# A router kernel fed by one stream of loads: spare products before four rows, an earlier table load, and a regrouped end of the stream

## The chip, the cores and the metric

The kernel runs on one core of a Trainium2 chip. The metric is the device time of one execution in microseconds (us); lower is better. A core has several engines that run side by side: TensorE (PE) multiplies matrices, with its weight loads shown apart as PEld; VectorE (DVE) and ScalarE (ACT) do elementwise work; GpSimd (POOL) here issues nearly all loads; SyncE (SP) here waits for loads and issues the stores. They are tied together by semaphores.

## The reference

```python
batch, seq, dim = 16, 512, 1024
num_loras = 8
# x: (16, 512, 1024) fp32, router_weights: (1024, 8) fp32

def reference(x, router_weights):
    logits = np.matmul(x, router_weights)
    exp_logits = np.exp(logits - np.max(logits, axis=-1, keepdims=True))
    return (exp_logits / np.sum(exp_logits, axis=-1, keepdims=True)).astype(np.float32)
```

x has 8192 rows of 1024 numbers, 33.5 MB in fp32. Each row is multiplied with an 8-column matrix and a softmax is taken over the 8 results. There is little arithmetic for each byte that is read.

## The kernel before

The 8192 rows are spread over 128 partitions, 64 to each. What the kernel and this text call "row j" is the j-th of these on every partition: a block of 128 rows of x. Row blocks 0 to 3 come in one fp32 load on the SyncE queue and are cast by ScalarE; blocks 4 to 62 come on the GpSimd queue in loads of several blocks, cast to bf16 by the DMA on the way; block 63 comes in three pieces of columns.

```python
    LOADS = [4] + [8] * 4 + [4] * 4 + [2, 2, 2] + [1] * 5     # blocks per load
    PIECES = [4, 2, 2]                                        # of block 63, in units of 128 columns
    G, SKIP = 8, 4
    TRIPS = 31
    ...
    place = [16640]                                           # next free address in SBUF
    ...
    X_AT = place[0]
    xa = sb("x_all", [P, J, D], bf16)
    x_f32 = sb("x_f32", [P, LOADS[0], D], fp32)
```

SyncE passes the landing of each load on, as a count of blocks that PE may take (semaphore s_in). GpSimd issues the loads one after the other, and they queue up:

```python
    for i, r in enumerate(LOADS):
        if i:
            sp.wait_ge(s_ld[i], 16)
            sp.sem_inc(s_in, r)
    ...
    for i, r in enumerate(LOADS):
        if i:
            nc.gpsimd.dma_start(
                out=xa[:, first[i]:first[i] + r, :], in_=x_rows[:, first[i]:first[i] + r, :]
            ).then_inc(s_ld[i], 16)
```

PE turns each block with eight transposes (through the identity) into PSUM. DVE copies five of the eight turned pieces to SBUF, ACT copies three, and PE multiplies them with the weights. PE runs this as a loop over two blocks. It turns the next block before it multiplies the present one, takes its instructions in order, and computes two "filler" products of 128x512 per trip whose result nobody reads:

```python
    def loop_turn(b):
        pe.wait_ge(s_in, 1).then_inc(s_in, -1)    # has the block landed?
        for c in range(KO):
            t = again(turn_like, ...)              # transpose at the address in register r_x[c]
            ...
        for c in range(KO):
            ...
            pe.reg_add(r_x[c], r_x[c], D * 2)      # on to the next block

    def fill():
        return pe.matmul(spare, lhsT=filler[:, 0:P], rhs=filler, start=True, stop=True)
    ...
    with nc.body("rows_multiply", valid_engines=only_pe):
        fill()
        fill()
        multiply(1, None)
        pe.br("rows_turn")
    with nc.body("rows_turn", valid_engines=only_pe):
        loop_turn(1)
        multiply(0, None)
        loop_turn(0)
        pe.br_lt(r_x[0], left_of(TRIPS - 1), on_true="rows_multiply", on_false="rows_done")
```

ScalarE waits for the first load before anything else. The load of its function table isn't written out here; it comes with the first cast and so stands behind that wait:

```python
    act.wait_ge(s_f, 16).then_inc(s_f, -16)
    for i in range(2):
        cast(i)
        for j in (2 * i, 2 * i + 1):
            act_copy(j, j)
```

After the loop, blocks 60 to 63 are finished alone: two multiplies, the three pieces of block 63, four small softmaxes, one last store.

Of the kernel before, what the change touches and what calls it, by code (L numbers as in the profile page):

```python
# [11 lines left out]
def kernel(  # L12
# [6 lines left out]
    nc = tc.nc  # L19
    P = 128  # L20
    B, S, D = x.shape
# [10 lines left out]
    fp32 = mybir.dt.float32  # L32
    bf16 = mybir.dt.bfloat16
    Exp = mybir.ActivationFunctionType.Exp
    X = mybir.AxisListType.X
    ALU = mybir.AluOpType

    LOADS = [4] + [8] * 4 + [4] * 4 + [2, 2, 2] + [1] * 5  # L40
    PIECES = [4, 2, 2]
    G, SKIP = 8, 4
    TRIPS = 31
# [5 lines left out]
    DONE = ends[-1]  # L49
    assert sum(LOADS) == J - 1 and sum(PIECES) == KO and ends[-1] == J - ALONE  # L50
    VN, SN = 5, 3

    place = [16640]

    def sb(name, shape, dtype):
        size = mybir.dt.size(dtype)
        for n in shape[1:]:
            size *= n
        at = place[0]
        place[0] = -(-(at + size) // 64) * 64  # L60
        return nc.alloc_sbuf_tensor_at(name, shape, dtype, offset=at).ap()
# [1 line left out]
    def ps(name, shape, dtype):  # L63
        return nc.alloc_psum_tensor(name, shape, dtype).ap()

    X_AT = place[0]
    xa = sb("x_all", [P, J, D], bf16)
    x_f32 = sb("x_f32", [P, LOADS[0], D], fp32)
    identity = sb("identity", [P, P], bf16)
    ident = sb("ident", [P, P], fp32)  # L70
    w8 = sb("w8", [KO, P, N], fp32)
# [31 lines left out]
    s_w = nc.alloc_semaphore("s_w")  # L103
    s_ld = [sem(f"s_ld{i}") for i in range(len(LOADS))]
    s_z = [sem(f"s_z{i}") for i in range(len(PIECES))]
# [21 lines left out]

    first = [sum(LOADS[:i]) for i in range(len(LOADS))]
    cols = [sum(PIECES[:i]) for i in range(len(PIECES))]


    with tc.manual_schedule():
        early = [
            nc.sync.dma_start(out=x_f32, in_=x_rows[:, 0:LOADS[0], :]).then_inc(s_f, 16),
            nc.scalar.dma_start(
# [25 lines left out]

    for j in range(LOADS[0]):
        sp.wait_ge(s_cast, j + 1)
# [34 lines left out]
    pe = nc.tensor  # L198
    r_x = [pe.alloc_register(f"rx{c}") for c in range(KO)]
    r_l = pe.alloc_register("rl")  # L200
    for c, r in enumerate(r_x):

        pe.reg_mov(r, X_AT + D * 2 + c * P * 2 + (P - 1) * 2)
    pe.reg_mov(r_l, LG_AT + 256 * (SKIP - 1))

    def at(ap, like, r):
        return mybir.RegisterAccessPattern(
            ap=ap, dtype=like.dtype, memsetref=like.tensor.name + "_set",
            regref=r.name, is_regloc_offset=False, reg_ap_offset=r.name,
            const_ap_offset=0, const_sub_tensor_id=0,  # L210
        )

    def again(like, **k):
        return pe.add_instruction(copy.replace(like, name=f"I-{nc.next_id()}", **k))

    def turn_ap(b, c):
        return (ptv if c < VN else pts)[b][:, c if c < VN else c - VN, :]

    def chunk(b, c):
        return xTv[b][:, c, :] if c < VN else xTs[b][:, c - VN, :]  # L220

    def loop_turn(b):

        pe.wait_ge(s_in, 1).then_inc(s_in, -1)  # L224
        for c in range(KO):
            t = again(
                turn_like,
                ins=(turn_like.ins[0], at([[J * D, P], [1, P]], xa, r_x[c])),
                outs=(pe.lower_ap(turn_ap(b, c), opt=False),),
            )  # L230
            if c == VN - 1:
                t.then_inc(s_tv, 1)
            if c == KO - 1:
                t.then_inc(s_ts, 1)
        pe.reg_add(r_l, r_l, 256)
        for c in range(KO):
            if c == KO // 2:
                pe.reg_alu(r_l, r_l, -4097, ALU.bitwise_and)
            pe.reg_add(r_x[c], r_x[c], D * 2)
# [10 lines left out]
    def multiply(b, dst):  # L250

        for c in range(KO):
            if c == 0:
                pe.wait_ge(s_c[b], 2).then_inc(s_c[b], -2)
            if dst is None:
                m = again(
                    mult_like,
                    ins=(
                        pe.lower_ap(w_bf[:, c, :], opt=False),
                        pe.lower_ap(chunk(b, c), opt=False, for_matmul_weights=True),  # L260
                    ),
                    outs=(at([[2 * G * 64, P], [1, N]], lg, r_l),),
                    start_tensor_calc=(c == 0),
                    stop_tensor_calc=(c == KO - 1),
                )
            else:
                m = pe.matmul(  # L267
                    dst, lhsT=chunk(b, c), rhs=w_bf[:, c, :],
                    start=(c == 0), stop=(c == KO - 1),
                )  # L270
            if c == KO - 1:
                m.then_inc(s_p, 1)

    def fill():
        return pe.matmul(spare, lhsT=filler[:, 0:P], rhs=filler, start=True, stop=True)  # L275
# [17 lines left out]
    def left_of(i):  # L293

        return X_AT + D * 2 * (2 * i + 3) + (P - 1) * 2

    only_pe = OrderedEngineSet([pe.engine])
# [6 lines left out]
    with nc.body("rows_turn", valid_engines=only_pe):  # L304
        loop_turn(1)
        multiply(0, None)
        loop_turn(0)
        pe.br_lt(r_x[0], left_of(TRIPS - 1), on_true="rows_multiply", on_false="rows_done")
    nc.switch_bb("rows_done")
# [32 lines left out]
    act = nc.scalar  # L342
# [14 lines left out]
    def act_copy(j, seen):  # L357

        act.wait_ge(s_ts, seen + 1)
        act.copy(xTs[j % 2], pts[j % 2][:, 0:SN, :]).then_inc(s_c[j % 2], 1)  # L360

    act.wait_ge(s_f, 16).then_inc(s_f, -16)  # L362
    for i in range(2):
        cast(i)
# [181 lines left out]
```

## Time and profile before

| | before |
|---|---|
| time, median of 3 runs | 85.58 us (85.53 to 85.76) |
| span of the profiled execution | 84.4 us |
| mean granted TensorE clock | 0.974 |
| PE busy | 62.4 us (74%) |
| DVE busy | 39.4 us (47%) |
| ACT busy | 38.0 us (45%) |
| read from HBM | 33.59 MB, 401 GB/s over the span |

The page of a profile has several parts. One shows the span in 40 equal slices (2.1 us each); a digit is the busy share in tenths, so 9 is 90% or more. "PEclk" is the clock that TensorE was granted, in the same tenths. A view of waits lists who waited for whom: total us, number of waits, the longest. "PEq" is PE's instruction sequencer: a wait put down to it is a wait on a semaphore at the line named. The view in order of time has start, duration, engine, line, operation, tiles and shapes; in brackets is the idle time before it and what ended it. The chain that ended last runs back from the last instruction, each step to what released it.

### The profile page before, as it was taken

The numbers are of one execution on the slowest core, as the hardware profiler recorded it, in microseconds if no ns is written. First come the engines' busy times: TensorE is split into PE (matmuls) and PEld (weight loads), VectorE is DVE, ScalarE is ACT, GpSimd is POOL, SyncE is SP. The second block draws the span as 40 slices with busy tenths as digits, with TensorE's granted clock in tenths as the row PEclk, the third lists the DMA queues.
The fourth block names the chain that finished last, engine by engine and source line by source line (L and its number), as shares of the span: only waits on it lengthen the run. The fifth ranks groups of instructions, "written<-read, shape, count | busy, mean of one in ns | idle before, by whom it ended". The sixth has DMA issues, their size and how long they took to land. (4 is left out here: it accounts for less than half of the span.)

```text
span 84.4 us, 2916 instructions
## 1 busy us (share of the span) xinstructions
PE 62.4 (74%) x1094; PEld 52.3 (62%) x1094; DVE 39.4 (47%) x114; ACT 38.0 (45%) x81; POOL 11.3 (13%) x26
## 2 busy tenths in 40 slices
PE   0070073999991999259990999999998799999870
PEld 0040072788871778238870688887887588777650
DVE  0030022247660685227660265678568357656662
ACT  0000988535460465225460254566546246546470
POOL 0699996000000000000000000000000000000000
PEclk9999999999999999999998579999999999999997
DMA  5999979997999799989998999999999999999930
GB/s 142 433 419 264 225 163 233 241 217 171 241 241 217 163 248 233 202 186 248 233 202 179 225 210 217 217 206 225 206 229 190 214 212 215 204 207 213 171 114 12
DMA packets 3184, 18.12 MB, mean 215 GB/s; under 512 B 488, under 2 KB 1000, under 8 KB 2032
## 3 DMA queue, kind: packets, MB, share of 16 engines
q0 software_dynamic: 2736, 15.73, 90.3%
q1 hardware_dynamic: 432, 2.36, 7.3%
q10 hardware_dynamic: 16, 0.03, 0.2%
HBM read 33.59 MB, written 0.26 MB: 401 GB/s over the span
## 5 line engine op out<-in xcount | busy, mean ns | idle before, releaser
L405 DVE COPY xTv<-ptv 128x640 bf16<-128x640 bf16 x63 | 31.0, 492 | 32.9 <-PE ptv L288 26.7
L360 ACT COPY xTs<-pts 128x384 bf16<-128x384 bf16 x63 | 30.1, 477 | 34.0 <-PE pts L288 33.6
L288 PE MATMUL ptv<-identity,x_all 128*128 128x128 bf16 x311 | 29.0, 226 | 14.4 <-PEq L224 9.5
L288 PEld LDWEIGHTS ptv<-identity,x_all 128*128 (+1 forms) x311 | 19.0, 99 | 15.4 <-issue 15.4
L288 PE MATMUL pts<-identity,x_all 128*128 128x128 bf16 x186 | 21.7, 228 | 0.0
L275 PEld LDWEIGHTS lg<-w_bf,xTv 128*128 128x128 bf16 x305 | 15.7, 98 | 7.9 <-issue 1.3
L275 PE MATMUL spare<-filler 128*128 128x512 bf16 x61 | 19.6, 402 | 0.2
L275 PE MATMUL lg<-w_bf,xTv 128*128 128x8 bf16 x305 | 16.7, 167 | 0.0
L288 PEld LDWEIGHTS pts<-identity,x_all 128*128 x186 | 13.9, 103 | 0.0
L275 PE MATMUL lg<-w_bf,xTs 128*128 128x8 bf16 x183 | 13.2, 166 | 0.0
L275 PEld LDWEIGHTS lg<-w_bf,xTs 128*128 128x128 bf16 x183 | 9.0, 96 | 0.0
L180 POOL DMA_DIRECT2D x_all<-in_x_dram x16 | 8.6, 588 | 2.2 <-POOLq L142 2.2
L275 PEld LDWEIGHTS spare<-filler 128*128 128x128 bf16 x61 | 4.7, 103 | 1.1 <-issue 1.0
L346 ACT ACT_TABLE_LOAD x1 | 1.3, 1283 | 8.5 <-ACTq L362 8.5
L282 PE MATMUL lg<-ident,w 8*128 8x8 f32 x8 | 1.0, 251 | 4.7 <-PEq L280 4.7
L346 ACT CAST x_all<-x_f 128x1024 bf16<-128x1024 f32 x4 | 4.0, 1044 | 0.0
L425 DVE TENSOR_REDUCE mx<-lg 128x8 f32 x8 | 1.8, 225 | 4.6 <-DVEq L475 4.1
L282 PEld LDWEIGHTS lg<-ident,w 8*128 8x128 f32 x8 | 0.9, 197 | 4.7 <-issue 4.7
L349 ACT ACTIVATE ev<-ex 128x64 f32<-128x64 f32 x8 | 2.1, 257 | 1.5 <-DVE ex L425 0.9
L396 DVE CAST identity<-ident 128x128 bf16<-128x128 f32 x1 | 0.5, 518 | 4.6 <-POOL ident L186 4.6
L441 DVE TENSOR_REDUCE ssum<-ev 128x8 f32<-128x64 f32 x8 | 1.7, 218 | 0.1
L425 DVE TENSOR_TENSOR ex<-lg,mx 128x64 f32<-128x64 f32 x8 | 1.7, 216 | 0.0
(41 smaller groups left out, 16.0 us busy)
## 6 DMA issues: line engine op xcount, KB each, us to landing
x_all<-in_x_dram POOLq DMA_DIRECT2D x4, 2048.0 KB, 27.7
x_all<-in_x_dram POOLq DMA_DIRECT2D x4, 1024.0 KB, 51.7
x_f<-in_x_dram SPq DMA_DIRECT2D x1, 2048.0 KB, 8.4
x_all<-in_x_dram POOLq DMA_DIRECT2D x3, 512.0 KB, 62.0
x_all<-in_x_dram POOLq DMA_DIRECT2D x5, 256.0 KB, 66.2
out_dram<-out_all SPq DMA_DIRECT2D x1, 240.0 KB, 2.0
x_all<-in_x_dram POOLq DMA_DIRECT2D x1, 128.0 KB, 67.8
x_all<-in_x_dram POOLq DMA_DIRECT2D x2, 64.0 KB, 67.5
```

What stands on the lines that cost most here:

```text
L180: nc.gpsimd.dma_start(out=xa[:, first[i]:first[i] + r, :], in_=x_rows[:, first[i]:first[i] + r, :]).then_inc(s_ld[i], 16)
L275: return pe.matmul(spare, lhsT=filler[:, 0:P], rhs=filler, start=True, stop=True)
L282: t = pe.transpose(w_ps[:, n, :], w8[:, :, n], ident[0:KO, 0:KO])
L288: turn_like = pe.transpose(turn_ap(0, 0), xa[:, 0, 0:P], identity).ins
L346: act.copy(xa[:, k, :], x_f32[:, k, :]).then_inc(s_cast, 1)
L349: return act.activation(ev, ex, func=Exp).then_inc(s_ev, 1)
L360: act.copy(xTs[j % 2], pts[j % 2][:, 0:SN, :]).then_inc(s_c[j % 2], 1)
L396: dve.tensor_copy(out=identity, in_=ident).then_inc(s_idb, 1)
L405: dve.tensor_copy(out=xTv[j % 2], in_=ptv[j % 2][:, 0:VN, :]).then_inc(s_c[j % 2], 1)
L425: return dve.add_instruction(kind(name=f"I-{nc.next_id()}", engine=dve.engine, **k))
L441: dve.reduce_sum(ssum[:, :, 0], ev, axis=X).then_inc(s_d, 1)
```

## The change

Three things are changed. Six spare products are put ahead of PE's wait for the first block of certain loads, so that PE isn't idle there and keeps its clock; a test of the address of the next block picks the place, and x_all is moved in SBUF so that a bit mask can do it. The function table of ScalarE is loaded before the wait for the first load. And blocks 52 to 62 come in loads of 3, 2, 2, 1, 1, 1, 1 in place of 2, 2, 2, 1, 1, 1, 1, 1.

```diff
-    LOADS = [4] + [8] * 4 + [4] * 4 + [2, 2, 2] + [1] * 5
+    LOADS = [4] + [8] * 4 + [4] * 4 + [3, 2, 2] + [1] * 4
...
+    LOT, SPARE = 8, 6
+    ROW_AT = 32 - LOADS[0] - LOT
+    assert LOADS[1:5] == [LOT] * 4 and 64 - ROW_AT == LOADS[0] + LOT * 5
...
-    X_AT = place[0]
+    x_f32 = sb("x_f32", [P, LOADS[0], D], fp32)
+    place[0] = X_AT = ROW_AT * D * 2
     xa = sb("x_all", [P, J, D], bf16)
-    x_f32 = sb("x_f32", [P, LOADS[0], D], fp32)
...
+    r_t = pe.alloc_register("rt")
...
         loop_turn(1)
         multiply(0, None)
+        pe.reg_alu(r_t, r_x[0], (64 + 32 + LOT - 1) * D * 2, ALU.bitwise_and)
+        pe.br_eq(r_t, 32 * D * 2, on_true="rows_spare", on_false="rows_even")
+    with nc.body("rows_spare", valid_engines=only_pe):
+        for _ in range(SPARE):
+            fill()
+        pe.br("rows_even")
+    with nc.body("rows_even", valid_engines=only_pe):
         loop_turn(0)
         pe.br_lt(r_x[0], left_of(TRIPS - 1), on_true="rows_multiply", on_false="rows_done")
...
+    act.preload_act_table(Exp)
     act.wait_ge(s_f, 16).then_inc(s_f, -16)
```

ROW_AT is 20: block j lies at (20 + j) x 2048 bytes, so the test looks at the bits of 20 + j.

## The prediction

> **What bounds the kernel now.** I read the page's slices first, then the queue totals, to see whether one resource is full all the time.
>
> ```profile
> PE   0070073999991999259990999999998799999870
> ...
> PEclk9999999999999999999998579999999999999997
> DMA  5999979997999799989998999999999999999930
> ...
> q0 software_dynamic: 2736, 15.73, 90.3%
> ```
>
> The DMA row stays at 9, with a few 7s and 8s, from the second slice until slice 38 of 40. PE has holes (a 1, a 2, a 0), each about one slice (2.1 us) wide. So the transfers set the pace and PE waits for them. Queue 0, the GpSimd queue with all loads of rows 4 to 63, carries nearly all of it.
>
> Next, the waits, the DMA queue's own included.
>
> ```profile
> SPq L168 <- DMA x_all<-in_x_dram: 63.6, 16, 9.7
> ```
>
> ```profile
> ACT xTs L360 <- PE pts L288: 33.6, 54, 3.1
> ...
> PE ptv L288 <- PEq L224: 9.5, 6, 2.5
> ACT L346 <- ACTq L362: 8.5, 1, 8.5
> ```
>
> SyncE waits 63.6 us for 16 loads of x, the longest for 9.7. L224 is PE's wait for a row to have come: six visible ones, 9.5 us in all, 2.5 at most. L362 is ScalarE's wait for the first four rows in fp32.
>
> The trace's completion marks of the loads give when each landed (us from the span's start): eight-row loads at 17.29, 26.97, 36.71, 46.38; four-row loads at 51.21, 56.08, 61.00, 65.85; two-row loads at 68.26, 70.73, 73.25; rows 58 to 62 at 74.47, 75.68, 76.93, 78.26, 79.49; the pieces of row 63 at 80.10, 80.45, 80.85. That is a stream without a hole: 9.70 us for eight rows (three steps: 9.69, 9.74, 9.67), 4.87 for four, 2.46 for two, 1.25 for one.
>
> PE in order of time shows where it stands to that stream.
>
> ```profile
> 24.93 0.22 PE L275 MATMUL lg<-w_bf,xTs 128*128 128x8 bf16 x3
> 27.14 0.44 PE L288 MATMUL ptv<-identity,x_all 128*128 128x128 bf16 x5 [1.99 <-PEq L224]
> ...
> 36.88 0.44 PE L288 MATMUL ptv<-identity,x_all 128*128 128x128 bf16 x5 [2.48 <-PEq L224]
> ...
> 46.55 0.69 PE L288 MATMUL ptv<-identity,x_all 128*128 128x128 bf16 x5 [2.41 <-PEq L224]
> 47.04 0.52 PE L288 MATMUL pts<-identity,x_all 128*128 128x128 bf16 x3
> 47.36 1.06 PE L275 MATMUL spare<-filler 128*128 128x512 bf16 x2
> ...
> 66.02 0.44 PE L288 MATMUL ptv<-identity,x_all 128*128 128x128 bf16 x5 [0.81 <-PEq L224]
> ...
> 79.66 0.44 PE L288 MATMUL ptv<-identity,x_all 128*128 128x128 bf16 x5 [0.41 <-PEq L224]
> ```
>
> These waits are for rows 12, 20, 28, 48 and 62, each ending 0.15 to 0.17 us after the landing of that row's load. At full clock a pair of rows with its two fillers takes 1.73 us (rows 36, 38, 40 and 42 start at 54.71, 56.43, 58.16, 59.89), 0.865 per row against the 1.21 that a row takes to arrive. At 46.55 the same five transposes take 0.69 instead of 0.44 and two fillers 1.06 instead of 0.59: the clock record falls to half at 45.98 and returns at 49.39.
>
> The chain that ended last starts at that last wait and ends with the last store.
>
> ```profile
> 79.62 0.04 issue
> 79.66 0.44 PE ptv L288 x5
> ...
> 82.75 0.19 DVE out_all L513
> ```
>
> So the end is the landing of row 62 and of the pieces of row 63 (80.85), then some 3.5 us of tail to 84.4. Whatever doesn't move those landings doesn't move the time.
>
> [...] eight rows are 8 x 128 x 4096 B = 4.19 MB of source in 9.70 us, 432 GB/s[...]. [...] by the steps above, each load costs only about 0.04 us beyond its rows.
>
> **The change, part by part.**
>
> *Early table load.* The load stands at 8.50 to 9.78, behind the wait for the first rows (landed 8.40), and the casts begin at 9.79. Moved ahead of the wait it runs while ScalarE has nothing to do (idle 8.50 us), so casts begin at 8.50 and PE's row 0 goes from 11.01 to about 9.73. But row 4 lands at 17.29 whatever PE does. PE turned it at 17.61; it can be 17.45 at the earliest. The 1.28 us shrink to about 0.16 at row 4 and to nothing at row 12, where PE waited 1.99.
>
> *Spare products.* The mask on the address picks even rows whose number plus 20 is 32, 40, 48 or 56: rows 12, 20, 28 and 36, so the branch is taken four times, with six products each, ahead of the wait for that row. At full clock fillers start 216 ns apart (two neighbours at 42.716 and 42.932), 6 x 0.216 = 1.30 us. For rows 12, 20 and 28 they lie in waits of 1.99, 2.48 and 2.41 and end 0.7 to 1.2 us before the row comes: no delay[...]. I expect the drop at 45.98 to be gone. It cost row 31 about 1.03 us (28 to 31: 46.55 to 50.60, 4.05; 20 to 23: 36.88 to 39.90, 3.02). For row 36 there is no wait to fill: the row landed at 51.21 and PE turned it at 54.71. There the six products are added work: 54.71 - 1.03 + 1.30 = 54.98, 0.27 later than before. Row 48 had 0.81 us of wait, so it still starts at 66.02. The compare and branch in every trip is PE's sequencer's work, which runs ahead; the existing branch (L308, median 208 ns) hides so. If 0.1 us of it showed in each of the 10 trips from row 28 to row 48, row 48 would come about 0.5 us late.
>
> *Loads of 3, 2, 2, 1, 1, 1, 1.* Row 52 now lands with 53 and 54: 65.85 + 3 x 1.2075 + 0.04 = 69.51. PE turned row 52 at 69.68 because it was busy with 48 to 51, so it needs it no earlier: 69.51 + 0.16 = 69.67. Rows 55 and 56 land near 71.97, 57 and 58 near 74.43, then 75.7, 76.9, 78.2 and row 62 at about 79.45. Eight loads become seven: one fixed cost less, 0.04 us (from 4.87 = f + 4r and 9.70 = f + 8r: r = 1.2075, f = 0.04). From row 48 at 66.02, fourteen rows at 0.865 bring PE to row 62 at 78.1; it has 1.5 us in hand against 79.6.
>
> Sum on the path that sets the end: 0 (table load) + 0 (spares) - 0.04 (one load fewer) = -0.04 us. 85.58 - 0.04 = 85.54.
>
> **Rivals.** *PE becomes the bound through row 36.* For it: PE is behind the stream from row 29 to row 47, and this is where unhidden work is added. Against it: the half clock avoided pays 1.03 of 1.30, the wait at row 48 has 0.81 and that at row 62 1.5 more. Even if the clock fell in spite of the spares (1.03 + 1.30 + 1.0 of branches), row 48 would be about 2.5 us late at worst and the end late by at most 1.0: 86.0 to 86.5. I give it 5%.
>
> *A starved PE at row 52.* It now starts a three-row burst only at 69.67. If it were already late there, rows 57 to 62 would press together at the end, 0.1 to 0.4 us. The page's even arrival rate speaks against it.
>
> *The stream itself changes.* The move of x_all to another address in SBUF, or a transfer of three rows (6 KB per partition instead of 4), could alter the rate. Only 0.1% in the steady rate of some 72 us would be 0.07 us, more than the gain. The source addresses don't change, and nothing in the trace speaks for it. I take it as the main part of the spread: +-0.1 us.
>
> *Every gain is real.* Were PE the bound, 1.28 + 1.03 + 0.04 would give 83.2. The chain of waits rules it out.
>
> **Range and chances.** Three runs of before lie between 85.53 and 85.76, so a median of few runs wanders by 0.1. With the spread of the stream and the small chance of a late row 62, I take 85.38 to 85.74. 2% is 1.7 us: nothing here shortens the stream so much, nor is any delay that large left after the slack at rows 48 and 62. Faster 0.01, within 2% 0.98, slower 0.01.
>
> **What would show it.** Table load near 3 to 4 us, first cast at about 8.5; PE's first row near 9.7, row 12 still near 27.1; six fillers before rows 12, 20, 28, 36, with a remaining wait of 0.6 to 1.2 before the first three; the clock row without its 8, 5, 7; row 36 turned close to 55.0; a wait at row 48 of about 0.5 and at 52 near none; row 62 near 79.6 and the tail of the same length. I am wrong if the last landing moves by more than 0.15 us, or if PE has no wait left before row 62.

## The result: slower by 1.7%

The changed kernel took 87.0 us (median of 6 runs, 86.9 to 87.12) beside 85.56 us for the kernel before (85.5 to 85.76). The ratio is 1.0167, 95% interval 1.0153 to 1.0182. The prediction was 85.54, with a range up to 85.74; the measured time is 1.26 us above the range.

The slices of the page after the change, in the same order as those of before:

```profile
PE   0070458699999999999997999999999999999960
...
PEclk9999999999999999999999999999999999999999
DMA  5999997999699979998898999999999999999420
```

The transfers now end early: the DMA row falls to 4 and 2 in slices 38 and 39, where before it held a 9 and a 3. PE has no hole after the eighth slice apart from one 7. The clock no longer falls: its record stands at full from 20.92 us to the end of the span. PE has become the bound. The chain that ended last says it too; before the change it held 2% of PE:

```profile
PE 39%; ACT 2%; DVE 1%; issue 1%
```

The waits of the changed kernel (total us, number, longest) show PE's wait for rows gone from 9.5 us to 2.7, and a new group: 25 short stops ahead of the two fillers of each trip, put down to "issue", that is to nothing which the profile shows.

```profile
PEld spare L283 <- issue: 5.4, 25, 0.2
...
PE ptv L296 <- PEq L232: 2.7, 3, 1.4
```

PE in order of time after the change, from row 36, from a trip later on (rows 40 to 42) and at row 62:

```profile
54.16 1.46 PE L283 MATMUL spare<-filler 128*128 128x512 bf16 x6
55.45 0.44 PE L296 MATMUL ptv<-identity,x_all 128*128 128x128 bf16 x5
...
59.21 0.44 PE L296 MATMUL ptv<-identity,x_all 128*128 128x128 bf16 x5
59.49 0.33 PE L296 MATMUL pts<-identity,x_all 128*128 128x128 bf16 x3
59.89 0.60 PE L283 MATMUL spare<-filler 128*128 128x512 bf16 x2
...
61.18 0.44 PE L296 MATMUL ptv<-identity,x_all 128*128 128x128 bf16 x5
...
80.74 0.44 PE L296 MATMUL ptv<-identity,x_all 128*128 128x128 bf16 x5
```

The same rows before the change, where the fillers follow the transposes without a gap:

```profile
58.16 0.44 PE L288 MATMUL ptv<-identity,x_all 128*128 128x128 bf16 x5
58.44 0.33 PE L288 MATMUL pts<-identity,x_all 128*128 128x128 bf16 x3
58.60 0.59 PE L275 MATMUL spare<-filler 128*128 128x512 bf16 x2
...
59.89 0.44 PE L288 MATMUL ptv<-identity,x_all 128*128 128x128 bf16 x5
```

After the change the eight transposes that begin at 59.21 are issued by 59.66 (the last three start 0.056 apart from 59.49), and the fillers start at 59.89: some 0.23 us of nothing, in nearly every trip. A trip of two rows takes 1.962 us, where it took 1.727 (from the sequencer's records in both traces, for trips at full clock in which PE had no row to wait for). Row 62 landed at 79.24, earlier than before (79.49), but PE turned it at 80.74, 1.5 us after it had come.

The gap itself lies over the branch that closes the loop (L323, in this trip from 59.62 to 59.83), and that branch is as old as the loop: it took as long before the change (L308, 207 or 208 ns in 29 of its 31 records), where PE still had instructions in hand while it ran (the branch from 58.31 to 58.51, transposes starting up to 58.55, the fillers at 58.60). What is new is the test, L316, some 0.8 us earlier in the trip. Both branches in the records of PE's sequencer (PEldq; ns, shortest/median/longest of 31):

```profile
L316 PEldq COMPARE_BRANCH  x31: 75/207/227, 11.6 to 80.4; - x31
L323 PEldq COMPARE_BRANCH  x31: 76/208/209, 13.6 to 81.1; - x31
```

The 75 ns of L316 belong to the four trips whose test runs straight on into the spare products, 207 (once 227) to the others, which jump over them. In the trip above, the sequencer reached the wait for row 40 at 59.09, only 0.12 us before PE turned that row (0.34 before the change, 57.82 to 58.16), so PE had next to nothing in hand when the closing branch came. Between the sequencer's two semaphore waits on either side of the test, 0.151 us passed before the change and 0.508 after it.

### The profile page after: what moved, and what is told of

Read it like the earlier page. It is cut to its first block, busy times and chain, and to the rows that moved or that the text cites. A ratio compares the mean times of both kernels' runs of the same rounds, so it can differ in the third digit from the quotient of the medians.

```text
span 85.6 us, 3024 instructions
## 1 busy us (share of the span) xinstructions
PE 70.7 (83%) x1118; PEld 54.4 (63%) x1118; DVE 39.1 (46%) x114; ACT 37.9 (44%) x81; POOL 10.8 (13%) x25
## 5 line engine op out<-in xcount | busy, mean ns | idle before, releaser
L283 PE MATMUL spare<-filler 128*128 128x512 bf16 x85 | 25.5, 396 | 1.1
L283 PEld LDWEIGHTS spare<-filler 128*128 128x128 bf16 x85 | 6.0, 100 | 7.3 <-issue 5.4
L187 POOL DMA_DIRECT2D x_all<-in_x_dram x15 | 8.1, 585 | 2.2 <-POOLq L149 2.2
```

Of the source, the lines that this page charges most:

```text
L187: nc.gpsimd.dma_start(out=xa[:, first[i]:first[i] + r, :], in_=x_rows[:, first[i]:first[i] + r, :]).then_inc(s_ld[i], 16)
```

## The experiments

**Theory A:** the test and its jump lengthen the way of PE's sequencer through a trip, so that the trip is as long as the sequencer needs and PE starves in it. **Theory B:** the 24 spare products, 0.216 us each, are the added work. **Theory C:** the moved x_all or the three-row load disturbs the stream. All times beside the kernel before in the same set of runs.

**Without the test and the spare products** (table load, move and loads stay).

```diff
         multiply(0, None)
-        pe.reg_alu(r_t, r_x[0], ...)
-        pe.br_eq(r_t, 32 * D * 2, on_true="rows_spare", on_false="rows_even")
-    with nc.body("rows_spare", ...): ...
-    with nc.body("rows_even", ...):
         loop_turn(0)
```

> The changed kernel without the test of the address and without the spare products; the table load, the move of x_all and the regrouped loads stay. Theory A (the test and its jump make PE's sequencer the bound: a trip of two rows 1.96 us in place of 1.73): the trip is back at 1.73, PE waits about 2 us before rows 12, 20 and 28, row 62 is turned when it lands, time 85.3 to 85.6. Theory B (the 24 spare products are added work): 85.3 to 85.6 too. Theory C (the moved x_all or the three-row load disturbs the stream): stays at 86.8 to 87.1.

Measured: 85.63 us, ratio 0.999 (0.9975 to 1.0005). PE's wait for rows is back:

```profile
PE ptv L296 <- PEq L232: 7.2, 7, 2.5
```

Theory C falls. The table load and the regrouped loads together are worth nothing that can be measured here.

**The test without spare products.**

```diff
     with nc.body("rows_spare", valid_engines=only_pe):
-        for _ in range(SPARE):
-            fill()
         pe.br("rows_even")
```

> The changed kernel with the test of the address and its jumps in every trip, but no spare product behind it. Theory A: a trip still takes 1.96 us, so from row 28 (landing near 46.2) 17 trips bring row 62 to about 46.3 + 33.4 = 79.7, 1.0 us before the changed kernel's 80.74 and some 0.3 after its landing: 85.8 to 86.2. Theory B: trips of 1.73 us, time 85.3 to 85.6.

Measured: 85.96 us, ratio 1.0056 (1.0033 to 1.008); trips of 1.962 us, as expected of A. B would have had 1.73. The 21 runs lie in two groups, 85.76 to 86.25 and 86.73 to 87.03. The profiled run, 86.89, is of the upper one, above A's 85.8 to 86.2, and its clock fell to half at 46.57 for 3.41 us. So without the spare products the clock can still fall at row 28, and in this run PE, with trips of 1.962 us and busy for 14.19 of the 14.5 us from 66.0 to 80.5, didn't win it back. Whether this divides the two groups stays open. One such fall takes about 0.02 off the mean clock of an 85 us span (an estimate: 0.5 x 3.41 / 85), and most runs of the lower group have a mean clock of 0.98 too. A fall alone then doesn't make a run long; it may matter where it comes.

**The spare products without a test: the loop cut into pieces.** Four loops, with straight trips between them that hold the products ahead of rows 12, 20 and 28; then a version with row 36 too.

```diff
-    with nc.body("rows_multiply", ...): ...     # one loop, with the test
+    for s, last in enumerate([t - 1 for t in SPARE_TRIPS] + [TRIPS - 1]):
+        ...                                      # the loop, up to trip `last`
+        spare_trip()     # fill, fill, multiply(1), loop_turn(1), multiply(0), 6 x fill, loop_turn(0)
```

> The changed kernel with the six spare products ahead of rows 12, 20 and 28, but placed by cutting the loop into four loops with a straight trip between them, so that no test is made; no spare products at row 36. Theory A: trips of 1.73 us, a wait of 0.4 to 1.2 us left before rows 12, 20 and 28, no fall of the clock, row 62 turned when it lands: 85.3 to 85.6. Theory B: 18 of the 24 spare products remain, so most of the loss remains: 86.4 to 86.8.

> As the one with three straight trips, and a fourth with six spare products ahead of row 36, where PE has no wait: all 24 products of the change, no test. Theory A: the 1.3 us at row 36 are won back before row 62 (14 to 17 trips at 1.73 us against 2.4 us of arrival), 85.3 to 85.6, the same as with three within 0.1. Theory B: as the changed kernel, 86.8 to 87.1.

Measured: 86.4 us (ratio 1.008, 1.0063 to 1.0098) and 86.47 (1.0085, 1.0068 to 1.0102). Both are well above A's 85.3 to 85.6. The first lies in B's range and the second below it, but the trips are what A said, 1.73 us, and the fourth set of products cost nothing that can be told from noise. In the version with four, row 36's six products are there, and PE still waits for row 48:

```profile
54.25 1.46 PE L283 MATMUL spare<-filler 128*128 128x512 bf16 x6
```

```profile
66.73 0.44 PE L296 MATMUL ptv<-identity,x_all 128*128 128x128 bf16 x5 [0.62 <-PEq L232]
```

What was late was the stream: the eight rows from 20 to 27 landed at 37.63 and 37.43, 10.67 and 10.76 us after the load ahead, where 9.70 is the rule, and everything behind them stayed late. Of the 16 completion marks of that load in the version with three, 15 had come by 36.70 and one came at 37.63. Both traces hold instruction transfers during the run, which neither the kernel before nor the changed kernel has: 16 KB each, at 31.34 and 51.17 us with products ahead of three rows, at 31.13, 51.08 and 60.90 with four. This gave **theory F**: the longer program is fetched during the run through the same DMA engines, and the load in flight waits for the engine that was taken away.

**The cut loops without any spare product.** The same program as the one with three straight trips, less the products.

```diff
         multiply(0, None)
-        for _ in range(SPARE):
-            fill()
         loop_turn(0)
```

> The loop cut into four loops with straight trips between them, as in the run with three straight trips, but without any spare product; rest as in the changed kernel. Theory F (the longer program makes PE fetch instructions during the run, 16 KB in about 0.95 us on one DMA engine, and the load in flight there ends that much later): two fetches, near 31 and 51 us, one load of x 0.8 to 1.1 us longer than its neighbours, time 86.2 to 86.6, as with the products. Theory B (the spare products made the cut loops slow): 85.4 to 85.7.

Measured: 86.38 us, ratio 1.0092 (1.0078 to 1.0107). The longest wait of SyncE for a load, 9.7 before and after the change, is 10.6:

```profile
SPq L175 <- DMA x_all<-in_x_dram: 65.5, 15, 10.6
```

and the queues in the half microsecond from 31.0 hold the fetch:

```profile
q0 software_dynamic: 10, 0.16, 153.4%
q8 instruction: 1, 0.02, 11.7%
```

One packet of 16 KB took 0.935 us on its engine; the load landed at 37.37, its other 15 marks by 36.48, 0.89 earlier. A second fetch at 51.79 moved the last landing only by tenths. My reading is that it made another engine late while the first still was, since the load above landed with the last of its 16 marks; why it cost so much less was not shown. Theory F holds. For the cut loops B has nothing left: the ratio to the kernel before is 1.008 with 18 products and 1.0092 without any.

**The jump turned round.** The same test and all 24 products, but the common outcome runs straight on and the four rare ones jump.

```diff
+    with nc.body("rows_spare", valid_engines=only_pe):      # now ahead of the loop
+        for _ in range(SPARE):
+            fill()
+        pe.br("rows_even")
     with nc.body("rows_multiply", valid_engines=only_pe):
     ...
         pe.br_eq(r_t, 32 * D * 2, on_true="rows_spare", on_false="rows_even")
-    with nc.body("rows_spare", ...): ...
     with nc.body("rows_even", valid_engines=only_pe):
```

> The changed kernel with the spare products moved out of the way: the common outcome of the test runs straight on (75 ns in the changed kernel's trace for the outcome that doesn't jump) and only the four trips with spare products jump (207 ns). All 24 products stay. Theory A (the sequencer's time counts): it saves about 0.1 to 0.15 us of the 0.40 us that the test adds to the sequencer in a trip, so a trip takes 1.82 to 1.90 us at full clock, row 62 is turned near its landing, time 85.5 to 86.2. Rival A2 (any test there empties PE's queue, whichever way it goes): trip 1.96, time 86.9 to 87.1.

Measured: 85.57 us, ratio 0.9999 (0.999 to 1.0009). The whole loss is gone, though the test runs in every trip and all 24 products are there. The test's branch now takes 75 ns in most trips:

```profile
L320 PEldq COMPARE_BRANCH  x31: 75/75/207, 11.8 to 78.8; - x31
```

The way between the two waits is 0.377 us, so the test adds 0.226 to it, where it added 0.357 with the jump (not the 0.40 of the expectation). The trip is 1.830 us, the gap ahead of the fillers 0.10 in place of 0.23, and PE waits for row 62 again:

```profile
58.76 0.44 PE L296 MATMUL ptv<-identity,x_all 128*128 128x128 bf16 x5
59.03 0.33 PE L296 MATMUL pts<-identity,x_all 128*128 128x128 bf16 x3
59.30 0.61 PE L283 MATMUL spare<-filler 128*128 128x512 bf16 x2
...
60.59 0.44 PE L296 MATMUL ptv<-identity,x_all 128*128 128x128 bf16 x5
```

```profile
79.48 0.44 PE L296 MATMUL ptv<-identity,x_all 128*128 128x128 bf16 x5 [0.20 <-PEq L232]
```

**The changed kernel without the two fillers of each trip.**

```diff
     with nc.body("rows_multiply", valid_engines=only_pe):
-        fill()
-        fill()
         multiply(1, None)
```

> The changed kernel, test and spare products included, without the two filler products in each trip, which is 0.43 us less work on PE per trip. Theory A (a trip is as long as the sequencer needs): a trip at full clock loses only the dispatch of four instructions, and takes 1.70 to 1.85 us, with PE idle in it 0.3 us or more. Rival (PE's own work sets the trip, the gap is a fixed bubble): 1.965 - 0.43 = 1.53 us. The clock may fall more often, so the time itself, 85.4 to 86.6, tells less than the trip.

Measured: 86.46 us, ratio 1.0101 (1.0086 to 1.0115). The trip is 1.942 us. PE lost 0.43 us of work and the trip 0.02. The rival's 1.53 is excluded; so is my own 1.70 to 1.85, which had put the dispatch of four instructions too high. PE now stands idle for about 0.3 us where the fillers were (the last transpose is issued by 61.33, the next product starts at 61.64), and for 0.16 at the test:

```profile
60.88 0.44 PE L296 MATMUL ptv<-identity,x_all 128*128 128x128 bf16 x5 [0.16 <-SPq L175]
61.16 0.33 PE L296 MATMUL pts<-identity,x_all 128*128 128x128 bf16 x3
61.64 0.27 PE L283 MATMUL lg<-w_bf,xTv 128*128 128x8 bf16 x5
```

The view names SyncE at 60.88, which passed on a later load at 60.86. This row, 42, had landed at 55.92; it is the sequencer that reached the wait only then.

**No test, the limit of the loop in a register.**

```diff
+    pe.reg_mov(r_e, left_of(4))
     ...
-        pe.br_lt(r_x[0], left_of(TRIPS - 1), on_true="rows_multiply", on_false="rows_done")
+        pe.br_lt(r_x[0], r_e, on_true="rows_multiply", on_false="rows_bound")
+    with nc.body("rows_bound", ...): ...   # on to rows_spare, or out when all trips are done
+    with nc.body("rows_spare", ...): ...   # most of a trip, with six products; then r_e is raised
```

> Spare products ahead of rows 12, 20 and 28 with no test added to a trip: the loop's own closing branch compares with a limit kept in a register, and a second copy of most of a trip holds the products. The rest is as in the changed kernel. Theory A: trips of 1.73 us, 85.4 to 85.65, a ratio to before of 0.998 to 1.001. If the second copy is enough for an instruction fetch during the run (theory F, of the cut loops): one load 0.9 to 1.0 us late, 86.3 to 86.5.

Measured: 85.97 us, ratio 1.0043 (1.003 to 1.0055), between the two expectations. The loop did as A said: no test and 151 ns between the waits, row 62 turned at 79.50. No load was late. But the step out of the loop cost PE 0.42 us right in the tail. It now takes two branches, and the second (L322) jumps over the second copy:

```profile
80.52 0.38 PE L348 MATMUL pts<-identity,x_all 128*128 128x128 bf16 x4 [0.42 <-issue]
```

In the sequencer's records the first branch runs on in 76 ns, from 79.88, and the second takes 345 ns, from 80.01, where the loop's own jumps take 207; the kernel before leaves its loop with one branch of 76 ns. Together they are the gap. Why this jump took longer stays open: a fetch of 16 KB shows only at 81.07, after the gap, so that the sequencer waited for its instructions isn't shown.

**Two tests, one behind the other, no spare products.**

```diff
         pe.reg_alu(r_t, r_x[0], ...)
-        pe.br_eq(r_t, 32 * D * 2, on_true="rows_spare", on_false="rows_even")
+        pe.br_eq(r_t, 32 * D * 2, on_true="rows_spare", on_false="rows_again")
+    ...
+        pe.reg_alu(r_t, r_x[0], ...)
+        pe.br_eq(r_t, 32 * D * 2, on_true="rows_spare2", on_false="rows_even")
```

> As the run with the test and no spare products, with a second, equal test and jump right behind the first in every trip. The first test lengthened the sequencer's way between its two semaphore waits from 0.151 to 0.508 us. Theory A (the trip is the sequencer's time): the second adds the same 0.357 again, a trip 1.962 + 0.357 = 2.32 us, row 62 near 46.4 + 17 x 2.32 = 85.8, time about 92 (91.4 to 92.8). Rival (a test costs one fixed gap in PE, however many instructions stand there): trip near 1.96, time 85.8 to 87.0.

Measured: 92.21 us in one run, the trip 2.323 us. The way between the two waits is 0.910, 0.402 more than with one test; the trip grew by 0.361, since the sequencer spent 0.04 less elsewhere in it. With two tests PE stands idle at the tests themselves, for 0.24 us ahead of each row that they guard:

```profile
62.84 0.44 PE L296 MATMUL ptv<-identity,x_all 128*128 128x128 bf16 x5 [0.24 <-PEq L232]
...
65.16 0.44 PE L296 MATMUL ptv<-identity,x_all 128*128 128x128 bf16 x5 [0.24 <-PEq L232]
```

**The kernel before without its fillers.** The two fillers of each trip are taken out of the kernel before, as they were out of the changed one.

> The kernel before without the two filler products of each trip (0.43 us of PE work). Theory A puts the sequencer's own length of a trip before the change at 1.962 - 0.357 = 1.605 us, and the fillers' share of it at about 0.02: so a trip at full clock takes 1.57 to 1.61 us, with PE idle in it, though its work is only 1.73 - 0.43 = 1.30. Rival: 1.30 to 1.35. The time isn't the point; the stream should hold it at 85.4 to 86.

Measured: 85.6 us in one run. At full clock its trips are 1.54 to 1.58 us, with PE idle in them:

```profile
53.48 0.44 PE L288 MATMUL ptv<-identity,x_all 128*128 128x128 bf16 x5
...
55.05 0.44 PE L288 MATMUL ptv<-identity,x_all 128*128 128x128 bf16 x5
...
56.60 0.44 PE L288 MATMUL ptv<-identity,x_all 128*128 128x128 bf16 x5
```

So the sequencer of the kernel before was never far ahead: with its fillers, worth 0.02 us to the sequencer, it needed about 1.6 us for a trip in which PE worked 1.727.

The account in one table, from the sequencer's records (us; full clock, trips without a wait for a row). The times come from several sets of runs, in which the kernel before took 85.56 to 85.7:

| kernel | between the waits beside the test | trip | time |
|---|---|---|---|
| before | 0.151 | 1.727 (PE's work) | 85.56 |
| before, no fillers | 0.151 | 1.54 to 1.58 | 85.6 |
| jump turned round | 0.377 | 1.830 | 85.57 |
| changed | 0.508 | 1.962 | 87.0 |
| changed, no fillers | 0.508 | 1.942 | 86.46 |
| test, no spare products | 0.508 | 1.962 | 85.96 |
| two tests | 0.910 | 2.323 | 92.21 |

From 0.377 to 0.508 is 0.131; from 1.830 to 1.962 is 0.132. In these kernels, once the sequencer was the bound, what was added to its way was added to the trip, to within 0.04 us.

## Why the prediction was wrong, point by point

**The step that failed** is this sentence of the part on spare products: "The compare and branch in every trip is PE's sequencer's work, which runs ahead; the existing branch (L308, median 208 ns) hides so." The existing branch was hidden because the sequencer had about 1.727 - 1.605 = 0.12 us a trip in hand (an estimate from the two traces: 1.605 = 1.962 - 0.357). The test took 0.508 - 0.151 = 0.357, so 0.235 of it showed in each trip. I had allowed 0.1, in ten trips, and only as an aside. The sentence took "runs ahead" for "has time to spare" and never set the sequencer's length of a trip beside PE's.

The prediction had one figure for a branch, the median of L308, 208 ns. The traces give 75 to 76 ns where a branch runs on (L308 too has one of 76, at its way out of the loop) and 207 to 208 in nearly all cases where it jumps, so one figure hides the difference that decided this case: 85.57 us with the jump turned round, 87.0 without.

**How 1.4 us come of it.** PE still turned row 28 as soon as it had come, at 46.33. From there to row 62 are 17 trips: 17 x 1.962 = 33.35, which gives 79.68. Row 36's six products add 6 x 0.216 = 1.30 less the gap of 0.235 that they fill: 1.06. That is 80.74, the measured start of row 62, where the kernel before had 79.66: 1.08 later. The tail from there to the end of the span was 4.90 instead of 4.76. Together 1.22 us of span, 84.4 to 85.6. The two profiled runs took 85.75 and 86.95 us, 1.20 apart; the rest of the 1.44 between the medians is that the profiled run of before was one of its longest.

**Neither part alone makes the loss.** The test without the products cost 0.26 us by the medians (85.96 beside 85.7), the products with a cheaper test nothing (85.57 beside 85.58). What row 36's products add can be won back in trips of 1.73 or 1.83 us, since a pair of rows arrives every 2.42, but not in trips of 1.962 before row 62 comes.

**The rival was the right one, at the wrong size.** "PE becomes the bound through row 36" had 5%, and 86.0 to 86.5. Its term for the branches, 1.0 us for ten trips to row 48, should have been 0.235 for each trip up to row 62, 4.0 us for 17; the "1.5 us in hand" at row 62 was counted with trips of 1.73. And row 36 alone isn't a cause: with trips of 1.73 its products cost nothing, as the cut loop with four sets shows. One of the signs that the prediction named came up as written: PE had no wait left before row 62. That the change stayed within 2%, to which I gave 0.98, was luck, for the slack at rows 48 and 62 on which the 0.98 rested was gone.

**The early table load** went as said: PE's row 0 at 9.65 (9.73 foretold), and nothing left of it later. **The spare products in the waits**: the clock did stay up, and none of the runs with spare products that was traced lost it between its rise and the tail (mean granted clock 0.994 to 1.0 in them, 0.974 before). But the rest of the wait, foretold as 0.6 to 1.2 us, was 0 for row 12 (turned at 27.49, 0.75 after landing), next to nothing for row 20 and 0.42 for row 28, since longer trips had eaten it (and, ahead of row 12, a clock that rose to full at 20.92 instead of 18.67). **Row 36** came at 55.45 (54.98 foretold), **row 48** at 67.04, 1.41 after its landing, where a wait of 0.5 was foretold.

**The regrouped loads**: from the landing of the first eight-row load to that of row 62 the stream took 62.21 us before and 62.17 after, 62.20 and 62.18 in the runs without the test and with the jump turned; the kernel before without fillers has 62.20. So 0 to 0.04, where 0.04 was foretold: it agrees, but is too small to be told from chance. The rest of the earlier landing (79.24 for 79.49) was there from the first eight-row load, 17.07 for 17.29, and such a shift is found between other runs too (17.14 in the kernel before without fillers).

**The full stream.** What shows that the stream was full is its even landings, 9.67 to 9.74 us for each eight rows, and queue 0's packets, which took 90.3% of the 16 DMA engines' span. The prediction's 432 GB/s count x as it is read, in fp32. Written as bf16 it is half of that (the profile of before has 215 GB/s in the mean for what the DMA engines moved), so that figure alone doesn't show it.

No version beat the kernel before: with the test out of the way or made cheap, the stream sets the end again, at 0.999 and 0.9999 of its time.

## What to carry to other kernels

Count a control instruction on the busiest engine against that engine's sequencer, not against its queue: add up the sequencer's own way through a loop trip and compare it with the work of the trip (here about 1.605 us, an estimate, beside 1.727); what is left is all that a new test may cost (0.12 us here, where the test took 0.357). Where a test must be, let the common outcome run straight on and the rare one jump (0.226 us for the test in place of 0.357 here). And unrolling wasn't the free way out: code that had to be fetched while a stream of loads filled the DMA engines made that stream late here, by 0.9 to 1.1 us.

## What the runs showed of the hardware that I had not expected

- A compare-and-branch of PE's sequencer took 75 or 76 ns where it ran on and mostly 207 or 208 where it jumped, and 345 in the one jump out of the loop of the run with the limit in a register; with the register operation ahead of it and what follows, a test added 0.226 us one way and 0.357 the other to the sequencer's way.
- Instructions fetched during the run came as single packets of 16 KB, 0.94 to 0.98 us on one of the 16 DMA engines in the cut loops. The eight-row load that was in flight then (16 completion marks) landed 10.6 to 10.8 us after the one ahead, where 9.70 was the rule, and the stream never got it back. With the stream as the bound, this cost 0.8 us of 85.6 in the cut loops without products.
- The clock fell to half during a single idle gap of PE of 2.41 us in the kernel before, while gaps of 1.99 and 2.48 us there passed without a fall. With a test but no spare products it fell at 46.57, just after a gap of 1.70 us. What decides which gap it falls in, no run here shows.
